# Prompt attention of a decoder step: inverse sums transposed and stored from GpSimd's queue, a third result buffer, operands prepared elsewhere in the half-step

## The chip, the cores and the metric

The kernel runs on one core of a Trainium2 chip. The metric is the device time of one execution in microseconds (us). TensorE (PE) multiplies and transposes, VectorE (DVE) and ScalarE (ACT) read its results from PSUM, GpSimd (POOL) works on SBUF, and DMAs are issued from the queues of SyncE (SP) and POOL.

## The reference

One step of a two-layer decoder for two groups that share the weights: a prompt of 1024 positions and 8 samples of 8 positions with a paged cache. Layer 0 is a pooling mixer and latent attention with 8 heads, then an MLP; layer 1 is a gated linear recurrence, then an MLP. The change touches the attention of layer 0. For the prompt it computes, for each of 8 heads with 96 elements per query and key:

```
s = (einsum(qn, k_nope) + einsum(qr, k_rope)) * 96 ** -0.5
s = where(key_pos <= query_pos, s, -inf)
p = softmax(s)
out = (p @ c) @ w_uv
```

All of it in float32. The samples have the same attention over 2048 cached positions each and 8 new ones.

## The kernel before, in words

Float32 accuracy comes from splitting each operand into a high and a low part of a narrower matmul type (`split`, L79 and L80) and adding three products (`mm3`, L136; the score and value products have their own loops).

`prompt_attention` works on 32 pieces, each a head h and a pair of query blocks ip, in the order 3, 0, 2, 1 within a head. Each piece takes two half-steps t, so a head takes eight, x = t % 8. The order of instructions on PE, DVE, ACT and POOL is the order in which this code issues them (`manual_schedule`); SP's queue is ordered by a scheduler. A half-step issues, in this order:

- `weigh`: ACT's exponential of the scores of the half-step before, L767, with the row sums written into `sm`.
- `prep` of the next head, in half-steps x = 4 to 7: four PE transposes of query or key rows into a bank `qkt`, ACT's high part (qth, L727, or kth, L730) and DVE's low part (ktl, L731). Part 0 also splits the head's values on POOL, `vt`, and, for every second head, issues from SP the loads of the query and key rows `qh` and `kh` (L691, L692) of the two heads after.
- `scores`: PE's score matmuls into one of two PSUM tiles `s` (L749), the causal mask (L752), and DVE's negated row maximum `nmx` (L755).
- `transposes` of earlier weights: PE (`ptp`, L794), ACT's high part `pTh` (L798), DVE's low part `pTl` (L799).
- `values`: PE's products with the values into `po` (L821), and, when a piece is complete, ACT's copy into the head's result buffer `ao` (L827), 128 x 1024. Its lower 64 partitions hold the high part's product and its upper 64 the low part's, which are to be added. There are two buffers `ao`.
- At x = 1, `inverses` of the head before: DVE's reciprocal `ri` of the row sums (L773), a DMA from SP that writes it to DRAM (`rs_d`, L774; its elements are not next to each other in DRAM), and a DMA from SP that reads it back, broadcast to all partitions (`rib`, L776).
- At x = 5, `finish` of the head before: POOL multiplies `ao` by `rib` (L780), SP stores the first 64 partitions into `mix_d` (L782), and POOL's queue adds the other 64 to the same rows by an accumulating DMA (L783), which waits for the store.

After the last head `sample_attention` begins: PE transposes the samples' queries and absorbs the key weights into them; `q4`, four copies of the rotary part of q, is made by POOL (L929) and transposed by PE (`q4t`, L934); a block-diagonal `qbd` is zeroed by POOL (L931) and filled by DVE (L936); POOL writes the mask `msk` of the new keys (L950 to L952), and DVE adds it to their scores (`snew`, L956). Then the cache is worked through page by page (128 pages): SP loads a page (`cp`, L892), PE transposes it (`cpt`, L973), DVE splits off its low part (`cl`, L977), PE forms the keys (`pk`, L136), and ACT copies its rotary scores (L1007).

Of the kernel before, what the change touches and what calls it, by code (L numbers as in the profile page):

```python
# [10 lines left out]
F32 = mybir.dt.float32  # L11
# [4 lines left out]
ALU = mybir.AluOpType  # L16
# [4 lines left out]
P = 128  # L21
D = 1024
KB = 8
SEQ = 1024
DB = 8
DT = 8
NS = DB * DT
# [3 lines left out]
H = 8  # L31
QN = 64
QR = 32
QH = 96
VH = 64
# [650 lines left out]
def load_heads(g, S, pl, hp, bufs):  # L686

    qt = pl.tile([P, 8, 2 * QH], F32, name="qh", tag="qh", bufs=bufs)
    kt = pl.tile([P, 8, 2 * QH], F32, name="kh", tag="kh", bufs=bufs)
    cols = slice(hp * 2 * QH, (hp + 1) * 2 * QH)  # L690
    g.nc.sync.dma_start(qt, S.q_d[:, cols].rearrange("(b p) d -> p b d", p=P))  # L691
    g.nc.sync.dma_start(kt, S.k_d[:, cols].rearrange("(b p) d -> p b d", p=P))  # L692
    return qt, kt


def prompt_attention(g, I, S, v_sb, first, mix0):
    nc = g.nc
    with ExitStack() as st:
        at = st.enter_context(pool(g, "at", 2, side="right"))
        ps = st.enter_context(pool(g, "ps3", space=PSUM))  # L700
# [5 lines left out]
        loaded = {0: first}  # L706
        heads = {}
        vts = {}
        ao = {}

        def prep(h, part):
            if part == 0:
                vt = vts[h] = at.tile([P, 8, 2, VH], F32R, name="vt", tag="vt")
                split(g, vt[:, :, 0], vt[:, :, 1], v_sb[:, :, h], nc.gpsimd)
                if h % 2 == 0 and h // 2 + 1 < 4:
                    loaded[h // 2 + 1] = load_heads(g, S, at, h // 2 + 1, 2)
                heads[h] = [at.tile([P, SEQ], F32R, name=nm, tag=nm) for nm in ("qth", "qtl", "kth", "ktl")]
            nm, hf = part // 2, part % 2
            src = loaded[h // 2][nm]
            th, tl = heads[h][2 * nm:2 * nm + 2]  # L720
            pt = ps.tile([P, 512], F32, name="qkt", tag="pt", bufs=3)
            for j in range(4):
                nc.tensor.transpose(pt[:QH, j * P:(j + 1) * P], src[:, hf * 4 + j, (h % 2) * QH:(h % 2 + 1) * QH], g.ident)
            cs = slice(hf * 512, (hf + 1) * 512)
            if nm == 0:

                nc.scalar.activation(th[:QH, cs], pt[:QH], AF.Copy, scale=SCALE)  # L727
                nc.vector.scalar_tensor_tensor(tl[:QH, cs], pt[:QH], SCALE, th[:QH, cs].bitcast(F32), ALU.mult, ALU.subtract)
            else:
                nc.scalar.copy(th[:QH, cs], pt[:QH])  # L730
                nc.vector.tensor_tensor(tl[:QH, cs], pt[:QH], th[:QH, cs].bitcast(F32), ALU.subtract)  # L731
# [27 lines left out]
        sums = {}  # L759
        rib = {}  # L760

        def weigh():
            h, i, sv, nm, nk = exps.pop(0)
            if h not in sums:
                sums[h] = g.tiny.tile([P, 8], F32, name="sm", tag="sm", bufs=2)
            p_ = at.tile([P, SEQ if i > 3 else 512], F32, name="p", tag="p" if i > 3 else "p4")
            nc.scalar.activation(p_[:, :nk], sv, AF.Exp, bias=nm, accum_out=sums[h][:, i:i + 1])  # L767
            P_[(h, i)] = p_

        def inverses(h):  # L770

            ri = g.tiny.tile([P, 8], F32, name="ri", tag="ri", bufs=2)
            nc.vector.reciprocal(ri, sums.pop(h))  # L773
            nc.sync.dma_start(S.rs_d[h].rearrange("(b p) -> p b", p=P), ri, allow_slow_non_contiguous=True)  # L774
            rib[h] = at.tile([P, SEQ], F32, name="rib", tag="rib", bufs=1)
            nc.sync.dma_start(rib[h], S.rs_d[h:h + 1].to_broadcast([P, SEQ]))  # L776

        def finish(h):
            o = ao.pop(h)
            nc.gpsimd.tensor_tensor(o, o, rib.pop(h), ALU.mult)  # L780
            rows = S.mix_d[512 + h * VH:512 + (h + 1) * VH, :SEQ]
            nc.sync.dma_start(rows, o[:VH])  # L782
            nc.gpsimd.dma_start(rows, o[VH:], accum_op=ALU.add)  # L783

        def transposes(h, ip, banks):

# [19 lines left out]
        def values(h, ip, banks):  # L806

            for b in banks:
                if b > ip:
                    continue  # L810
                if b == 0:
                    PO[h, ip] = ps.tile([P, 512], F32, name="po", tag="po", bufs=1)
                po = PO[h, ip]
                parts = PT.pop((h, ip, b))
                for jj in range(2):
                    j = 2 * b + jj
                    lone = j == 2 * ip + 1
                    out = po[:, P:2 * P] if lone else po[:, :2 * P]
                    cs = slice(2 * P, 3 * P) if lone else slice(jj * 2 * P, (jj + 1) * 2 * P)
                    for x, t in enumerate(parts):  # L820
                        nc.tensor.matmul(out, vts[h][:, j].rearrange("p s d -> p (s d)"), t[:, cs],  # L821
                                         start=(j == 0 and x == 0), stop=(lone and x == 1))
            if ip not in banks:
                return
            if h not in ao:
                ao[h] = at.tile([P, SEQ], F32, name="ao", tag="ao", bufs=2)
            nc.scalar.copy(ao[h][:, ip * 2 * P:(ip + 1) * 2 * P], PO.pop((h, ip))[:, :2 * P])  # L827

        for q in range(4):
# [3 lines left out]
        N = len(seq)  # L833
        ET = mybir.EngineType
        with g.tc.manual_schedule(engines={ET.PE, ET.DVE, ET.Activation, ET.Pool}):
            for t in range(2 * N + 6):
                n, half = divmod(t, 2)
                if exps:
                    weigh()
                if n < N:  # L840
                    h, ip = seq[n]
                    if h + 1 < H and n % 4 >= 2:
                        prep(h + 1, 2 * (n % 4 - 2) + half)
                    scores(h, 2 * ip + 1 - half)

                m, back = divmod(t - 3, 2)
                if 0 <= m < N:
                    transposes(*seq[m], (2, 3) if back else (0, 1))
                m, back = divmod(t - 4, 2)
                if 0 <= m < N:  # L850
                    values(*seq[m], (2, 3) if back else (0, 1))
                hd, x = divmod(t, 8)
                if x == 1 and hd:
                    inverses(hd - 1)
                elif x == 5 and hd:
                    finish(hd - 1)

def sample_attention(g, I, S, ahead, fill_start, fill):  # L860
    nc = g.nc
    SQ = H * DT
    with ExitStack() as st:
# [38 lines left out]
        pt = one("qst", "ct")  # L902
# [5 lines left out]
        for h0 in range(0, H, 2):  # L908
            pt = one("wkt", "up" if h0 % 4 else "dn", 2)
# [5 lines left out]
        for k in range(2):  # L915
            pt = one("qap", ("up", "dn")[k], 2)
# [9 lines left out]
            WQ.append(wq)  # L926

        q4 = sk.tile([P, H, 4, QR], F32, name="q4", bufs=1)
        nc.gpsimd.tensor_copy(q4[:NS], S.q_s[:NS, :, None, QN:].to_broadcast([NS, H, 4, QR]))  # L929
        qbd = sk.tile([P, DB, 4, H, DT], F32, name="qbd", bufs=1)  # L930
        nc.gpsimd.memset(qbd, 0.0)  # L931
        pt = msc("q4t")
        for h in range(H):
            nc.tensor.transpose(pt[:, h * NS:(h + 1) * NS], q4[:NS, h].rearrange("p a b -> p (a b)"), g.ident[:NS, :NS])  # L934
# [730 lines left out]
```

## Time and profile before

| | us |
|---|---|
| median of 3 runs | 2814.39 |
| lowest and highest | 2813.95, 2814.64 |
| the profiled execution | 2802.13 |
| its span | 2800.2 |

Over the span PE is busy 2670.9 us (95%), DVE 1771.8 (63%), ACT 923.6 (33%) and POOL 405.3 (14%). The prompt's attention is the part from 240 to 414 us.

In a timeline a row has the start, the length, the engine, the line, the operation with its output and inputs, the count, and in brackets the idle time of the engine before it and what ended that. PEld is PE's weight load. "SPq" and "POOLq" are queues' own rows. In a row of waits the numbers are the total, the count and the longest. PEclk is the granted clock of PE as a share of 2.4 GHz; 0.5 is its lower level of 1.2 GHz.

### The profile page before, as it was taken

What the parts mean: (1) busy time and instruction counts of PE and PEld (TensorE: products, weight loads), DVE (VectorE), ACT (ScalarE), POOL (GpSimd) and SP (SyncE); (2) the same over time, 40 slices, a digit from 0 to 9 for tenths busy, and PEclk for the clock granted to TensorE, in tenths of its full rate; (3) what the DMA queues carried; (4) which work ended last, traced back from release to release, by engine and by line L of the source; (5) the groups of instructions that cost most, each with busy time, mean ns of one, the idle gap of its engine ahead of it and who ended that gap; (6) DMA issues with size and microseconds to landing.
All of it is one profiled execution on the core that took longest, in us unless ns stands there. A gap on an engine that the chain in (4) does not pass through costs nothing.

```text
span 2800.2 us, 42502 instructions
## 1 busy us (share of the span) xinstructions
PE 2670.9 (95%) x16513; PEld 2584.3 (92%) x16513; DVE 1771.8 (63%) x3323; ACT 923.6 (33%) x1948; POOL 405.3 (14%) x459
## 2 busy tenths in 40 slices
PE   7998987999989999999999999999999999999999
PEld 6887877888879999999999988998999999999998
DVE  7666655788855555555555577997555555555555
ACT  5335764666644111111111135664411111111111
POOL 4221211322332000000000033444200000000000
PEclk9999998999999999999999999999999999999999
DMA  5233443222152111111111111113111111111101
GB/s 162 61 113 117 73 50 83 67 55 55 42 148 69 42 42 46 46 46 46 46 46 40 44 69 56 43 41 110 55 39 45 46 46 46 46 46 46 39 30 64
DMA packets 207859, 168.34 MB, mean 60 GB/s; under 512 B 48987, under 2 KB 189244, under 8 KB 206883
## 3 DMA queue, kind: packets, MB, share of 16 engines
q1 hardware_dynamic: 207019, 163.54, 19.7%
q0 software_dynamic: 640, 2.10, 1.2%
q8 instruction: 130, 2.13, 0.3%
q14 instruction: 70, 0.57, 0.1%
HBM read 142.37 MB, written 23.34 MB: 59 GB/s over the span
## 4 chain that ended last, share of the span: by engine, by line
PE 62%; DVE 7%; ACT 1%; DMA 1%; issue 1%; POOL 0%; ACTq 0%; DVEq 0%; POOLq 0%
PE up L136 27%; PE dn L136 26%; PE op L136 5%; PE pu L136 2%; DVE xl L182 1%; DVE v L1386 1%; PE pgt L136 1%; DVE ig L1401 1%; DVE hs L1417 0%; DMA raw<-mix_d 0%; DVE t L1402 0%; DVE y L250 0%; DVE ta L1404 0%; DVE xl L80 0%; PE otp L1596 0%
## 5 line engine op out<-in xcount | busy, mean ns | idle before, releaser
L250 DVE TENSOR_TENSOR y<-y,dn 128x384 f32<-128x384 f32 (+1 forms) x768 | 405.1, 531 | 282.1 <-PE dn L136 279.6
L136 PE MATMUL dn<-hh,whB 128*128 128x384 f32 (+1 forms) x1536 | 506.7, 330 | 3.9 <-DVE y L250 3.8
L136 PE MATMUL up<-xh,wlA 128*128 128x384 f32 (+1 forms) x1536 | 502.4, 327 | 0.0
L136 PE MATMUL dn<-hh,wlB 128*128 128x384 f32 (+1 forms) x1536 | 501.9, 327 | 0.0
L136 PE MATMUL up<-xh,whA 128*128 128x384 f32 (+1 forms) x1536 | 501.8, 327 | 0.0
L136 PE MATMUL up<-xl,whA 128*128 128x384 f32 (+1 forms) x1536 | 501.7, 327 | 0.0
L136 PE MATMUL dn<-hl,whB 128*128 128x384 f32 (+1 forms) x1536 | 501.6, 327 | 0.0
L79 ACT CAST whB<-raw 128x1024 fp32r<-128x1024 f32 (+3 forms) x80 | 80.0, 1035 | 699.5 <-PE dn L136 663.7
L136 PEld LDWEIGHTS dn<-hh,whB 128*128 128x128 f32 x1536 | 288.5, 188 | 11.9 <-DVE y L250 11.6
L136 PEld LDWEIGHTS up<-xh,wlA 128*128 128x128 f32 x1536 | 288.5, 188 | 0.4
L136 PEld LDWEIGHTS up<-xh,whA 128*128 128x128 f32 x1536 | 288.6, 188 | 0.3
L136 PEld LDWEIGHTS dn<-hl,whB 128*128 128x128 f32 x1536 | 288.6, 188 | 0.1
L136 PEld LDWEIGHTS up<-xl,whA 128*128 128x128 f32 x1536 | 288.5, 188 | 0.2
L136 PEld LDWEIGHTS dn<-hh,wlB 128*128 128x128 f32 x1536 | 288.6, 188 | 0.0
L235 DVE SCALAR_TENSOR_TENSOR rl<-up,rs 128x384 f32<-128x384 f32 (+1 forms) x192 | 102.8, 535 | 260.5 <-PE up L136 260.5
L236 ACT ACTIVATE hh<-rl 128x384 fp32r<-128x384 f32 (+1 forms) x192 | 97.1, 506 | 447.7 <-DVE rl L235 447.7
L80 POOL TENSOR_TENSOR wlA<-raw,whA 128x1024 fp32r<-128x1024 f32 (+2 forms) x24 | 58.1, 2422 | 745.8 <-ACT whA L79 745.8
L136 PE MATMUL pk<-wqh,cl 128*128 128x256 f32 (+1 forms) x512 | 153.3, 305 | 12.8 <-DVE cl L977 12.7
L136 PE MATMUL pk<-wqh,ch 128*128 128x320 f32 (+1 forms) x512 | 160.0, 315 | 0.7 <-ACT ch L976 0.7
L79 ACT CAST whA<-raw 128x1024 fp32r<-128x1024 f32 (+2 forms) x94 | 98.0, 1043 | 181.5 <-PE up L136 143.2
L237 DVE TENSOR_TENSOR rl<-rl 128x384 f32<-128x384 f32 (+1 forms) x192 | 106.0, 552 | 77.4 <-ACT hh L236 77.4
L136 PE MATMUL pk<-wql,ch 128*128 128x256 f32 (+1 forms) x512 | 151.8, 298 | 0.0
(561 smaller groups left out, 5324.8 us busy)
## 6 DMA issues: line engine op xcount, KB each, us to landing
raw<-in_w_up_dram SPq DMA_DIRECT2D x64, 512.0 KB
raw<-in_w_down_dram SPq DMA_DIRECT2D x64, 512.0 KB
cp<-in_cache_ckv_dram SPq DMA_DIRECT2D x128, 128.0 KB
raw<-in_w_in_rnn_dram SPq DMA_DIRECT2D x16, 512.0 KB
xt<-in_x_prompt_dram SPq DMA_DIRECT2D x8, 512.0 KB
raw<-in_w_out_even_dram SPq DMA_DIRECT2D x8, 512.0 KB
raw<-in_x_prompt_dram SPq DMA_DIRECT2D x8, 512.0 KB
rib<-rs_d SPq DMA_DIRECT2D x8, 512.0 KB
```

The costliest lines, as they stand in the source:

```text
L79: g.nc.scalar.copy(h, src)
L80: (lo or g.nc.vector).tensor_tensor(l, src, h.bitcast(F32), ALU.subtract)
L136: g.nc.tensor.matmul(ps, a, b, start=(i == 0), stop=(i == n - 1))
L182: nc.vector.scalar_tensor_tensor(xl[:, m], yv, gcol[:, m:m + 1], xh[:, m].bitcast(F32), ALU.mult, ALU.subtract)
L235: nc.vector.scalar_tensor_tensor(r[:, :n], ps[:, :n], 0.0, RS[c][:, :n], ALU.max, ALU.mult)
L236: nc.scalar.activation(hh[:, a:b], r[:, :n], AF.Square)
L237: nc.vector.tensor_tensor(r[:, :n], r[:, :n], r[:, :n], ALU.mult)
L250: nc.vector.tensor_tensor(y[c][:, m], y[c][:, m], ps[:, :n], ALU.add)
L1386: V.scalar_tensor_tensor(v, ul[:, a + k:b + k], vec[:, k, n:n + 1], v, ALU.mult, ALU.add)
L1401: V.scalar_tensor_tensor(t2, t2, 1.0, v, ALU.add, ALU.mult)
```

## The change

The inverse sums are transposed by PE into a bank `rit` of the PSUM tag that the other transposes use, copied out by DVE as `riT` (8 x 128), and written to DRAM from POOL's queue in rows of 128; the broadcast load of them is issued from POOL's queue too. `sm` and `ri` come from the loop's own pool. There are three buffers `ao`. `prep` of the next head stands at the end of half-steps x = 3 to 6, behind `values`, no longer ahead of `scores` in x = 4 to 7. The loads of query and key rows have one buffer each and are issued behind the last transposes of an odd head. `finish` stands at x = 4, and the accumulating DMA at x = 7; the last head's first store goes to POOL's queue as well. For the samples, the copy `q4` is made by ACT and `qbd` is zeroed by DVE.

```diff
--- before.py
+++ after.py
@@ -712,8 +712,6 @@
             if part == 0:
                 vt = vts[h] = at.tile([P, 8, 2, VH], F32R, name="vt", tag="vt")
                 split(g, vt[:, :, 0], vt[:, :, 1], v_sb[:, :, h], nc.gpsimd)
-                if h % 2 == 0 and h // 2 + 1 < 4:
-                    loaded[h // 2 + 1] = load_heads(g, S, at, h // 2 + 1, 2)
                 heads[h] = [at.tile([P, SEQ], F32R, name=nm, tag=nm) for nm in ("qth", "qtl", "kth", "ktl")]
             nm, hf = part // 2, part % 2
             src = loaded[h // 2][nm]
@@ -721,6 +719,8 @@
             pt = ps.tile([P, 512], F32, name="qkt", tag="pt", bufs=3)
             for j in range(4):
                 nc.tensor.transpose(pt[:QH, j * P:(j + 1) * P], src[:, hf * 4 + j, (h % 2) * QH:(h % 2 + 1) * QH], g.ident)
+            if part == 3 and h % 2 and h < H - 1:
+                loaded[h // 2 + 1] = load_heads(g, S, at, h // 2 + 1, 1)
             cs = slice(hf * 512, (hf + 1) * 512)
             if nm == 0:
 
@@ -762,25 +762,31 @@
         def weigh():
             h, i, sv, nm, nk = exps.pop(0)
             if h not in sums:
-                sums[h] = g.tiny.tile([P, 8], F32, name="sm", tag="sm", bufs=2)
+                sums[h] = at.tile([P, 8], F32, name="sm", tag="sm", bufs=2)
             p_ = at.tile([P, SEQ if i > 3 else 512], F32, name="p", tag="p" if i > 3 else "p4")
             nc.scalar.activation(p_[:, :nk], sv, AF.Exp, bias=nm, accum_out=sums[h][:, i:i + 1])
             P_[(h, i)] = p_
 
         def inverses(h):
 
-            ri = g.tiny.tile([P, 8], F32, name="ri", tag="ri", bufs=2)
+            ri = at.tile([P, 8], F32, name="ri", tag="ri", bufs=2)
             nc.vector.reciprocal(ri, sums.pop(h))
-            nc.sync.dma_start(S.rs_d[h].rearrange("(b p) -> p b", p=P), ri, allow_slow_non_contiguous=True)
+            pt = ps.tile([P, 512], F32, name="rit", tag="pt", bufs=3)
+            nc.tensor.transpose(pt[:8, :P], ri, g.ident)
+            riT = at.tile([8, P], F32, name="riT", tag="riT", bufs=1)
+            nc.vector.tensor_copy(riT, pt[:8, :P])
+            nc.gpsimd.dma_start(S.rs_d[h].rearrange("(b p) -> b p", p=P), riT)
+
+        def spread(h):
             rib[h] = at.tile([P, SEQ], F32, name="rib", tag="rib", bufs=1)
-            nc.sync.dma_start(rib[h], S.rs_d[h:h + 1].to_broadcast([P, SEQ]))
+            nc.gpsimd.dma_start(rib[h], S.rs_d[h:h + 1].to_broadcast([P, SEQ]))
 
         def finish(h):
             o = ao.pop(h)
             nc.gpsimd.tensor_tensor(o, o, rib.pop(h), ALU.mult)
             rows = S.mix_d[512 + h * VH:512 + (h + 1) * VH, :SEQ]
-            nc.sync.dma_start(rows, o[:VH])
-            nc.gpsimd.dma_start(rows, o[VH:], accum_op=ALU.add)
+            (nc.sync if h < H - 1 else nc.gpsimd).dma_start(rows, o[:VH])
+            return rows, o
 
         def transposes(h, ip, banks):
 
@@ -823,7 +829,7 @@
             if ip not in banks:
                 return
             if h not in ao:
-                ao[h] = at.tile([P, SEQ], F32, name="ao", tag="ao", bufs=2)
+                ao[h] = at.tile([P, SEQ], F32, name="ao", tag="ao", bufs=3)
             nc.scalar.copy(ao[h][:, ip * 2 * P:(ip + 1) * 2 * P], PO.pop((h, ip))[:, :2 * P])
 
         for q in range(4):
@@ -839,8 +845,6 @@
                     weigh()
                 if n < N:
                     h, ip = seq[n]
-                    if h + 1 < H and n % 4 >= 2:
-                        prep(h + 1, 2 * (n % 4 - 2) + half)
                     scores(h, 2 * ip + 1 - half)
 
                 m, back = divmod(t - 3, 2)
@@ -850,10 +854,15 @@
                 if 0 <= m < N:
                     values(*seq[m], (2, 3) if back else (0, 1))
                 hd, x = divmod(t, 8)
+                if hd + 1 < H and 3 <= x <= 6:
+                    prep(hd + 1, x - 3)
                 if x == 1 and hd:
                     inverses(hd - 1)
-                elif x == 5 and hd:
-                    finish(hd - 1)
+                    spread(hd - 1)
+                elif x == 4 and hd:
+                    done = finish(hd - 1)
+                elif x == 7 and hd or t == 2 * N + 5:
+                    nc.gpsimd.dma_start(done[0], done[1][VH:], accum_op=ALU.add)
 
 
 
@@ -926,9 +935,9 @@
             WQ.append(wq)
 
         q4 = sk.tile([P, H, 4, QR], F32, name="q4", bufs=1)
-        nc.gpsimd.tensor_copy(q4[:NS], S.q_s[:NS, :, None, QN:].to_broadcast([NS, H, 4, QR]))
+        nc.scalar.copy(q4[:NS], S.q_s[:NS, :, None, QN:].to_broadcast([NS, H, 4, QR]))
         qbd = sk.tile([P, DB, 4, H, DT], F32, name="qbd", bufs=1)
-        nc.gpsimd.memset(qbd, 0.0)
+        nc.vector.memset(qbd, 0.0)
         pt = msc("q4t")
         for h in range(H):
             nc.tensor.transpose(pt[:, h * NS:(h + 1) * NS], q4[:NS, h].rearrange("p a b -> p (a b)"), g.ident[:NS, :NS])
```

PE where half-step x = 1 ends and the next begins (`rit` is the transpose of the inverse sums of the head before). Before:

```order
L794 MATMUL ptp<-ident,p 128x128 x7
L821 MATMUL po<-pTh,vt 128x256
L821 MATMUL po<-pTl,vt 128x256
L821 MATMUL po<-pTh,vt 128x128
L821 MATMUL po<-pTl,vt 128x128
L749 MATMUL s<-kth,qth 128x256
L749 MATMUL s<-ktl,qth 128x256
```

Now:

```order
L800 MATMUL ptp<-ident,p 128x128 x7
L827 MATMUL po<-pTh,vt 128x256
L827 MATMUL po<-pTl,vt 128x256
L827 MATMUL po<-pTh,vt 128x128
L827 MATMUL po<-pTl,vt 128x128
L775 MATMUL rit<-ident,ri 8x128
L749 MATMUL s<-kth,qth 128x256
```

Between the values and the next scores there is now one transpose, which reads DVE's `ri`.

ACT in half-steps x = 6 and 7 (`kth` is the high part of the next head's keys, `p` the exponential). Before:

```order
L827 COPY ao<-po 128x256
L767 ACTIVATE p,sm<-s,nmx 128x640
L730 CAST kth<-qkt 96x512
L827 COPY ao<-po 128x256
L767 ACTIVATE p,sm<-s,nmx 128x512
L730 CAST kth<-qkt 96x512
L798 CAST pTh<-ptp 128x512 x2
```

Now:

```order
L833 COPY ao<-po 128x256
L730 CAST kth<-qkt 96x512
L767 ACTIVATE p,sm<-s,nmx 128x640
L833 COPY ao<-po 128x256
L730 CAST kth<-qkt 96x512
L767 ACTIVATE p,sm<-s,nmx 128x512
L804 CAST pTh<-ptp 128x512 x2
```

Each cast of `kth` has moved from behind an exponential to ahead of it.

POOL at the end of the prompt's attention and the start of the samples'. Before:

```order
L780 TENSOR_TENSOR ao<-ao,rib 128x1024
L783 DMA mix_d<-ao 64x1024
L929 COPY q_4781<-q_s 64x1024
L931 MEMSET qbd 128x2048
L950 MEMSET msk 64x64
```

Now:

```order
L778 DMA rs_d<-riT 8x128
L782 DMA rib<-rs_d 128x1024
L786 TENSOR_TENSOR ao<-ao,rib 128x1024
L788 DMA mix_d<-ao 64x1024
L865 DMA mix_d<-ao 64x1024
L959 MEMSET msk 64x64
```

The copy of q and the zeroing have left POOL's order, and the write of the inverses, their broadcast load and the last head's first store have come into it. On SP's queue the load of the page table (`ptb`) and those of the cache pages now stand directly behind the store of head 6.

## Rows read from the trace of the kernel before

**Rows 1.** Windows in prompt attention and at the start of the samples'.

```profile
core 0: us, PE busy (x) PEld busy (x) DVE busy (x) ACT busy (x) POOL busy (x), PEclk, DMA share, GB/s
...
308.00:329.00 21.00, 20.16 (x149) 17.52 (x148) 15.24 (x27) 16.31 (x39) 4.52 (x3) 1.00 0.31 59
415.00:436.00 21.00, 6.61 (x63) 6.22 (x61) 5.53 (x10) 4.49 (x10) 4.75 (x4) 0.66 0.28 51
436.00:450.00 14.00, 12.61 (x77) 11.18 (x76) 7.55 (x14) 5.97 (x19) 5.40 (x12) 0.65 0.41 106
```

**Rows 2.** Reciprocals of the row sums on DVE: summary of the line, then its timeline.

```profile
L773 DVE RECIPROCAL ri<-sm x8: 191/192/195, 265.4 to 413.8; 128x8 f32<-128x8 f32 x8
285.09 0.19 DVE L773 RECIPROCAL ri<-sm 128x8 f32<-128x8 f32 x1
308.84 0.19 DVE L773 RECIPROCAL ri<-sm 128x8 f32<-128x8 f32 x1
328.21 0.19 DVE L773 RECIPROCAL ri<-sm 128x8 f32<-128x8 f32 x1
347.60 0.19 DVE L773 RECIPROCAL ri<-sm 128x8 f32<-128x8 f32 x1
372.57 0.19 DVE L773 RECIPROCAL ri<-sm 128x8 f32<-128x8 f32 x1
```

**Rows 3.** Waits of ACT from 240 to 415 us: total, times, longest.

```profile
ACT ao L827 <- DMA mix_d<-ao: 15.8, 3, 5.7
```

**Rows 4.** Timelines of POOL, SP's queue and ACT around the first stall.

```profile
285.12 0.98 POOL L783 DMA_DIRECT2D mix_d<-ao  x1 [3.49 <-DMA mix_d<-ao]
285.31 0.38 SPq L774 DMA_DIRECT2D rs_d<-ri  x1
297.97 0.37 ACT L827 COPY ao<-po 128x256 f32<-128x256 f32 x1 [5.11 <-DMA mix_d<-ao]
```

**Rows 5.** POOL's accumulating stores, line 783: issue durations in ns, and landing.

```profile
L783 POOL DMA_DIRECT2D mix_d<-ao x8: 846/861/983, 285.1 to 433.6; - x8
DMA to landing us min/median/max: 3.9/7.1/12.7
```

**Rows 6.** Window behind the third stall.

```profile
404.70:411.60 6.90, 6.64 (x29) 6.33 (x30) 2.50 (x4) 4.16 (x11) 2.35 (x1) 0.51 0.34 97
```

**Rows 7.** Timeline of PE in an undisturbed head, half-step x = 1.

```profile
327.06 0.33 PE L749 MATMUL s<-kth,qth 96*128 96x256 f32 x1
```

**Rows 8.** Timelines of ACT, PE, weight loads, undisturbed head, x = 7 and 0.

```profile
339.83 0.69 ACT L767 ACTIVATE p<-s,nmx 128x512 f32<-128x512 f32 x1 [1.14 <-DVE nmx L755]
340.66 0.51 PE L749 MATMUL s<-kth,qth 96*128 96x512 f32 x1 [0.63 <-ACT p L767]
341.85 0.19 PEld L749 LDWEIGHTS s<-ktl,qth 96*128 96x128 f32 x1 [0.42 <-DVE ktl L731]
```

**Rows 9.** Timeline of ACT at the start of the loop.

```profile
251.00 1.05 ACT L79 CAST whA<-raw 128x1024 fp32r<-128x1024 f32 x1 [0.53 <-DMA raw<-in_w_out_even_dram]
```

**Rows 10.** Timelines of SP's queue, POOL, PE and DVE at the end.

```profile
414.00 0.37 SPq L774 DMA_DIRECT2D rs_d<-ri  x1
422.92 0.33 SPq L776 DMA_DIRECT2D rib<-rs_d  x1
427.85 2.33 POOL L780 TENSOR_TENSOR ao<-ao,rib 128x1024 f32<-128x1024 f32 x1 [14.48 <-DMA rib<-rs_d]
433.57 0.86 POOL L783 DMA_DIRECT2D mix_d<-ao  x1 [3.40 <-DMA mix_d<-ao]
435.54 1.11 PE L934 MATMUL q4t<-ident,q 64*128 64x64 f32 x8 [14.39 <-POOL q L929]
442.03 0.67 DVE L956 TENSOR_TENSOR snew<-snp,msk 64x512 f32<-64x512 f32 x1
```

**Rows 11.** Copy of the rotary scores, one per page of the cache.

```profile
L1007 ACT COPY s<-pk x128: 201/207/258, 446.2 to 766.5; 128x64 f32<-128x64 f32 x128
```

**Rows 12.** Timeline of POOL, a value split.

```profile
288.91 1.28 POOL L80 TENSOR_TENSOR vt<-v_sb,vt 128x512 fp32r<-128x512 f32 x1 [2.81 <-PE s L752]
```

## Prediction

> **What bounds the kernel now.** I read the page first (the slices, then the costliest groups), then the windows over prompt attention, the waits of ACT in it, the timelines of the engines at four places, and the queue waits. In an undisturbed head TensorE is the bound: in 21.0 us PE is busy 20.16, DVE 15.24, ACT 16.31, at full clock [rows 1]. A head then takes 19.4 us, read from one reciprocal of the row sums to the next: 328.21 − 308.84 = 19.37 and 347.60 − 328.21 = 19.39 [rows 2]. Two heads are longer, 308.84 − 285.09 = 23.75 and 372.57 − 347.60 = 24.97. There ACT's copy of the result waits for a DMA: three such waits, 15.8 us in all [rows 3], one of them 5.11 us [rows 4]. That is the wait for the result buffer of the head before last, whose accumulating store is still going. The store that delays it was issued at 285.12, beside the write of the inverse sums at 285.31 [rows 4], which goes out as 1024 single elements; the same pairing stands at the other two. POOL's accumulates land after 3.9 us at the least and 12.7 at the most [rows 5].
>
> At the end, after the last head, PE idles 14.39 us for POOL's copy of q [rows 10]. POOL is late because a chain of transfers stands before that copy: inverse sums out at 414.00, broadcast issued at 422.92, multiply at 427.85, accumulate at 433.57. The clock sinks there: granted 0.66 from 415 to 436 and 0.65 from 436 to 450 (1.0 is 2.4 GHz, 0.5 is 1.2) [rows 1].
>
> **The change part by part.** Sums are made against the profiled execution of 2802.13 us; the median of the runs is 2814.39, 12.26 more, and I carry the same shift over.
>
> A, **the three ACT stalls go**, for two reasons at once: the third buffer gives each accumulate a whole head more, and the 1024-element write is replaced by an 8x128 one with rows of 512 B. The first two are worth the excess of their heads over 19.38: 4.37 + 5.59 us, clock loss included. The third falls in the last head, which prepares no successor, so there is no equal to compare. By the ratio of the first two (9.96 us for 15.8 − 5.7 = 10.1 us of wait) it is 5.6; at the upper end it is 5.7 and half of the 6.9 us that follow at half clock [rows 6], 9.1. I take 6.7, nearer to the measured ratio. A = −16.6, ends −14 (buffers free somewhat late still) and −19.
>
> B, **PE waits for the reciprocal.** The transpose of the inverses stands on PE behind the values and ahead of the next scores. On a clean head PE began those scores at 327.06 [rows 7], while DVE's reciprocal began at 328.21 and took 0.19 [rows 2]: PE would stand until 328.40, so 1.3 us, eight times at most. The last of them stands ahead of work for the samples that may be late anyway: 0.8. The transpose itself is one short matmul, nothing beside this. B = 7 × 1.3 + 0.8 = +9.9. Ends: +4, where half is taken out of waits that PE has in the same head (21.0 − 20.16 = 0.84 per window), and +13, where copies behind it on DVE come 0.4 later each time. DVE's copy of 8x128 is no longer than its reciprocal row, since PE doesn't wait for it.
>
> C, **operands prepared at the end of half-steps.** ACT's cast of a half of kth now stands ahead of the exponential. Before, that exponential waited 1.14 us for DVE's maximum, and the cast came after it; so PE stood 0.63 for the scores' bank and its weight load 0.42 for ktl [rows 8]. Both holes, 1.05 us, should close, in 7 heads, −7.4; with a little from the queries' half I take −7.7. Ends: 0 (the hole moves to the maximum of the scores) and −9. The moved loads of query and key rows run while PE works, and have more than half a head before their first use: nothing, and a late one would show as a wait of PE's transposes.
>
> D, **the start.** ACT's first cast of the output weights, which waited 0.53 us for its load [rows 9], now stands ahead of the first copies of transposed weights: +1, ends 0 and +2.5 (the wait and two casts of 1.05).
>
> E, **the junction.** The copy of q goes to ACT, the zeroing to DVE, both idle there. The 14.39 us of PE's wait go. What is late next: the first page's latent rows, whose loads SP can now issue during the last head, since no write of that head is on its queue. Low end: the 10.7 us from 435.54 [rows 10] to the first page's output at 446.2 [rows 11] run at full clock too and take half, −14.4 − 5.3 = −19.7. High end: without a pause of its own PE goes three pages at half clock, each 2.52 us longer ((766.5 − 446.2)/127 [rows 11]), −14.4 + 7.6 = −6.8. I take −14.0, nearest to the wait that is measured.
>
> F, **POOL's and SP's queues.** Per head POOL now has 3.9 for the write of inverses (the least of its landings [rows 5], as no element-wise write is beside it), 4.93 from issue of the broadcast to the multiply, 2.33, 3.40 for the store, 0.86 for the accumulate [rows 10] and 1.28 for the value split [rows 12]: 16.7 us of 19.4. It fits, so it costs nothing; SP loses two issues and two long waits per head.
>
> Sum: −16.6 + 9.9 − 7.7 + 1.0 − 14.0 = −27.4; 2802.1 − 27.4 = 2774.7 profiled, and 2814.4 − 27.4 = **2787.0** for the median.
>
> **Rivals.** 1: *the order's gain does not come and PE's wait is longer* (C = 0, B = +13): −16.6 + 13 + 1 − 14 = −16.6, 2797.8. For it: PE has only 0.84 us of slack per window, so each hole that opens is paid for. Against: both holes of rows 8 end with instructions that the new order puts earlier.
>
> 2: *DVE stands at the mask.* The mask of the new keys is set by POOL, now behind the last head's whole chain; DVE's masked sums, at 442.03 before [rows 10], need it and stand ahead of the next split of latent rows. With F's terms the mask comes 17 us after the last reciprocal (413.8), and the sums' turn comes after PE's 7.4 us (435.54 − 14.39 = 421.15, less 413.79) and three pages of 2.5 to 5 us, so 16 to 24 after it: no wait or 1. If the write took the 8.92 us of before (422.92 − 414.00), the mask would be 5 later: up to +5, 2791.
>
> 3, the slower side: *POOL falls behind.* Its last chain ends at 265.4 [rows 2] + 8 × (time per head). Over (442.0 − 265.4)/8 = 22.1 us per head DVE's masked sums come later than they did before, and the kernel is slower. Were the write and the broadcast each to land in the 12.7 us that POOL's slowest accumulate took [rows 5], a head would take 12.7 + 12.7 + 2.33 + 3.40 + 0.86 + 1.28 = 33.3, the chain would end at 532, some 90 us late: 2904. Against it: the slow landings stand beside element-wise writes, which are gone; and POOL's eight issues took 846 to 983 ns [rows 5] while DVE was busy 15.24 of 21 us.
> The Trainium skill speaks for this rival ("SBUF — State Buffer", sections "SBUF: two separate sides" and "A bandwidth-pool intuition that's wrong"): a DMA issued from GpSimd's queue needs its descriptors written by GpSimd, which is shut out while VectorE runs an instruction in a two-port mode; the page measures 620 ns alone and 3100 ns beside such a copy, and advises SP's or ACT's queue. By that, an estimate from the page is 2.5 us more for each of three issues, 24.2 per head, past the point of 22.1 and about +17 us. The trace does not agree so far: its eight issues spread over 0.14 us.
>
> 4: *the stalls only move*, because the multiply and store come later with a slower chain: A = 0, so −10.8, 2803.6; with rival 1 on top it is 0, no change.
>
> **Chances.** Forecast 0.58, rival 1 0.19, rival 2 0.12, rival 3 0.05, rival 4 alone 0.03, with rival 1 0.03. A difference under 0.2% (5.6 us) can't be told from none here. Faster: 0.58 + 0.19 + 0.12 + 0.03 = 0.92, same 0.03, slower 0.05. The range goes up past rival 1 to 2802, and down by 14 of the 16.3 us that the low ends add up to (A 2.4, B 5.9, C 1.3, D 1.0, E 5.7), as all of them at once are unlikely: 2773. That leaves out rivals 3 and 4 and the far ends.
>
> **What would show it.** In the new profile: no wait of ACT's result copy for a DMA (A); a PE wait of about 1.3 us for the reciprocal in each head, and heads of 19.4 + 1.3 − 1.1 = 19.6 us (B, C); no hole of PE at the two scores of rows 8 (C); PE going on within 2 us of the last values, q's transposes without a wait for POOL (E); accumulates landing in about 4 us and POOL's multiply within 10 us of the reciprocal (F). Heads near 21 us mean rival 1; a DVE wait for the mask, rival 2; ACT waits for the accumulate that return in later heads, rival 3 or 4. Wrong altogether it is if the masked sums run later than 442 us.

## The result and the profile after

The changed kernel takes 2777.69 us (median of 4 runs, 2772.78 to 2778.56) against 2814.51 before (2813.95 to 2814.70): a ratio of 0.9866, 95% interval 0.9849 to 0.9883, or 36.8 us less. The forecast was 27.4 less, 2787.0 with a range of 2773 to 2802: the direction and the range held, the size was a quarter short. The profiled execution of the changed kernel took 2777.03 us, as the timed ones do.

The reciprocals of the row sums in the changed kernel, the summary of the line (compare [rows 2]):

```profile
L773 DVE RECIPROCAL ri<-sm x8: 193/194/195, 266.3 to 397.1; 128x8 f32<-128x8 f32 x8
```

and four of them in DVE's timeline:

```profile
285.48 0.20 DVE L773 RECIPROCAL ri<-sm 128x8 f32<-128x8 f32 x1
304.69 0.19 DVE L773 RECIPROCAL ri<-sm 128x8 f32<-128x8 f32 x1
323.86 0.20 DVE L773 RECIPROCAL ri<-sm 128x8 f32<-128x8 f32 x1
343.02 0.19 DVE L773 RECIPROCAL ri<-sm 128x8 f32<-128x8 f32 x1
```

The six heads that prepare a successor take 19.17 us each (343.02 − 323.86 is 19.16, 304.69 − 285.48 is 19.21), and the last, which prepares none, 15.79; no long head is left. From the first reciprocal to the last it is 397.15 − 266.31 = 130.8 us, where it was 148.3.

The waits of PE in the changed kernel, from 230 to 445 us: total, times, longest:

```profile
PE rit L775 <- DVE ri L773: 10.7, 8, 1.4
PE ptp L800 <- DVE pTl L805: 5.2, 1, 5.2
PE pk L136 <- DVE wql L80: 3.7, 1, 3.7
PE s L749 <- ACT p L767: 1.6, 2, 1.2
```

The new wait for the reciprocal is there eight times, 1.33 us each. The wait for the scores' bank, 4.7 us in seven before, is 1.6 in two. The 14.39 us for POOL's copy of q [rows 10] are gone; in their place stand 3.7 for DVE's low part of the key weights. One more wait, 5.2 us at the start, belongs to ACT, whose timeline there shows it:

```profile
248.01 1.04 ACT L79 CAST whA<-raw 128x1024 fp32r<-128x1024 f32 x1 [5.36 <-DMA raw<-in_w_out_even_dram]
```

ACT stands 5.36 us for the output weights, where it stood 0.53 [rows 9]. Its waits list has no row any more for a result copy that waits for the accumulate [rows 3]. The accumulates in the view of their line (issue in ns, then landing):

```profile
L865 POOL DMA_DIRECT2D mix_d<-ao x8: 887/893/899, 281.3 to 411.6; - x8
...
DMA to landing us min/median/max: 3.9/4.1/4.4
```

and the new write of the inverses in that of its own:

```profile
L778 POOL DMA_DIRECT2D rs_d<-riT x8: 556/562/709, 267.6 to 398.4; - x8
...
DMA to landing us min/median/max: 1.6/2.5/3.5
```

All eight accumulates land within 4.4 us, where three took over 10 and the slowest 12.7 [rows 5].

At the end of the prompt's attention, the timeline of PE:

```profile
405.54 0.71 PE L943 MATMUL q4t<-ident,q 64*128 64x64 f32 x8
412.75 0.90 PE L136 MATMUL pk<-wql,ch 128*128 128x320 f32 x2 [3.70 <-DVE wql L80]
```

that of DVE:

```profile
421.95 0.68 DVE L965 TENSOR_TENSOR snew<-snp,msk 64x512 f32<-64x512 f32 x1
```

and the copies of the rotary scores, one per page (compare [rows 11]):

```profile
L1016 ACT COPY s<-pk x128: 202/207/260, 417.7 to 738.1; 128x64 f32<-128x64 f32 x128
```

PE transposes q without a wait, 8.4 us after the last reciprocal (405.54 − 397.15). The first page is done 20.55 us after it (417.7 − 397.15), where it took 446.2 − 413.8 = 32.4 [rows 2, 11]. DVE's masked sums don't wait for the mask.

**The profiled execution of before was a short one.** From it to the profiled execution of after the time falls by 25.1 us only, while the medians differ by 36.8. So the kernel before was profiled twice more:

> The kernel before, unchanged, profiled again. Theory (the profiled execution of 2802 had fewer stalls than the timed ones of 2807 to 2816): one with 2808 to 2815 shows four to six waits of ACT's result copy for the accumulate, about 5 us each, in place of three. Rival: three waits again, and the time lies in other parts, as PE's clock in the MLPs.

> The same once more. Theory and rival as for the first: the time goes with the number of waits of ACT's result copy, or it doesn't.

They took 2814.46 and 2813.62 us, as the timed runs do. The theory was wrong: ACT's waits for the accumulate are 16.6 us in three and 18.1 in four, hardly more than the 15.8 of [rows 3], and from the first reciprocal to the last it is 148.3 and 148.0 us again. In the first of the two, the reciprocals:

```profile
L773 DVE RECIPROCAL ri<-sm x8: 192/194/195, 269.8 to 418.1; 128x8 f32<-128x8 f32 x8
```

the copies per page:

```profile
L1007 ACT COPY s<-pk x128: 203/207/259, 455.3 to 776.1; 128x64 f32<-128x64 f32 x128
```

ACT's timeline at the start and PE's at the end:

```profile
255.32 1.05 ACT L79 CAST whA<-raw 128x1024 fp32r<-128x1024 f32 x1 [2.06 <-DMA raw<-in_w_out_even_dram]
```

```profile
444.65 1.11 PE L934 MATMUL q4t<-ident,q 64*128 64x64 f32 x8 [18.67 <-POOL q L929]
```

The difference lies at both ends, not in the heads. The end is 455.3 − 418.1 = 37.2 us where [rows 2, 11] give 32.4, with a wait for q of 18.67 in place of 14.39; the first reciprocal is 4.3 us later, of which 2.7 were already there at a DVE row ahead of the loop (L564, 221.74 against 219.04) and 1.5 come from the longer wait for the output weights. Against this ordinary execution the change reads, in us:

| stretch | before, again | after | change | forecast |
|---|---|---|---|---|
| up to the first reciprocal | 269.8 | 266.3 | −3.4 | −0.1 (D, one head of C) |
| first reciprocal to last | 148.3 | 130.8 | −17.5 | −14.1 (A, six heads of C, seven of B) |
| last reciprocal to first page | 37.2 | 20.6 | −16.7 | −13.2 (E, the last of B) |
| the rest | 2357.3 | 2357.6 | +0.3 | 0 |
| span | 2812.6 | 2775.3 | −37.3 | −27.4 |

One of C's seven heads falls into the first stretch, because head 0 prepares head 1 before its own row sums are inverted.

### The profile page after: what moved, and what is told of

Same layout as the page of the kernel before. It is cut to its first block, busy times and chain, and to the rows that moved or that the text cites. A ratio compares the mean times of both kernels' runs of the same rounds, so it can differ in the third digit from the quotient of the medians.

```text
span 2775.3 us, 42539 instructions
## 1 busy us (share of the span) xinstructions
PE 2663.1 (96%) x16521; PEld 2580.4 (93%) x16521; DVE 1781.6 (64%) x3332; ACT 924.0 (33%) x1949; POOL 412.2 (15%) x474
## 3 DMA queue, kind: packets, MB, share of 16 engines
q1 hardware_dynamic: 197467, 159.05, 19.4%
## 4 chain that ended last, share of the span: by engine, by line
PE 64%; DVE 7%; ACT 1%; issue 1%; DMA 0%; POOL 0%; ACTq 0%; DVEq 0%; SPq 0%; POOLq 0%
PE up L136 27%; PE dn L136 27%; PE op L136 6%; PE pu L136 2%; DVE xl L182 1%; PE pgt L136 1%; DVE v L1395 1%; DVE ig L1410 1%; DVE hs L1426 0%; DVE y L250 0%; DVE t L1411 0%; PE pg L136 0%; DVE xl L80 0%; PE otp L1605 0%; DVE ta L1413 0%
## 5 line engine op out<-in xcount | busy, mean ns | idle before, releaser
L136 PEld LDWEIGHTS dn<-hh,whB 128*128 128x128 f32 x1536 | 288.3, 188 | 13.4 <-DVE y L250 13.1
L136 PE MATMUL pk<-wqh,cl 128*128 128x256 f32 (+1 forms) x512 | 153.6, 306 | 12.7 <-DVE cl L986 12.6
```

The lines of the kernel that those rows point to most:

```text
L136: g.nc.tensor.matmul(ps, a, b, start=(i == 0), stop=(i == n - 1))
```

## The experiments

Behind each time stand, in brackets, its ratio to the kernel before, which ran beside it, and the 95% interval of that ratio. The kernel before had medians of 2811.67 to 2812.59 us there, 2 to 3 us less than in the section on the result. So a difference to the changed kernel's 2777.69 us is uncertain by about 3 us, and the stretches of the traces are read with it. Of the longer edits only the lines that matter are shown; "..." marks what is left out.

**Two buffers or three.** The changed kernel with two result buffers.

```diff
-                ao[h] = at.tile([P, SEQ], F32, name="ao", tag="ao", bufs=3)
+                ao[h] = at.tile([P, SEQ], F32, name="ao", tag="ao", bufs=2)
```

> The changed kernel with two result buffers again. Theory (the form of the write removed the stalls): in the changed kernel head 0's accumulate is issued at 281.32 us and should land some 4 us later, while the buffer is next needed about 7.8 us after the second reciprocal (285.48), near 293; two buffers are enough, so no wait of ACT's result copy for a DMA and 2778 us, within 3. Rival (the third buffer removed them): waits of about 5 us come back in several heads, 2788 to 2808.

2777.17 us (0.9879, 0.9864 to 0.9894), the same as with three; no wait of ACT for the accumulate, heads of 19.1 us. Its accumulates:

```profile
DMA to landing us min/median/max: 3.9/4.2/4.7
```

With the new write the third buffer is worth nothing.

**The third buffer alone**, in the kernel before.

```diff
-                ao[h] = at.tile([P, SEQ], F32, name="ao", tag="ao", bufs=2)
+                ao[h] = at.tile([P, SEQ], F32, name="ao", tag="ao", bufs=3)
```

> The kernel before with a third result buffer and nothing else. Theory (either the buffer or the form of the write would have taken the stalls away): no wait of ACT's result copy for a DMA, heads of 19.4 us throughout, the end as before: 16 us less than before, 2797. Rival (the slow accumulates delay something else, the next loads or POOL's chain): the waits move, 2803 to 2813.

2796.58 us (0.9947, 0.9934 to 0.9960): 15 less than the 2811.67 of before beside it. All heads are 19.4 us, 398.0 − 267.1 = 130.9 in all, although the accumulates stay slow. The views of the accumulate's line, of the reciprocal's, and of PE's waits:

```profile
DMA to landing us min/median/max: 4.1/9.4/12.4
```

```profile
L773 DVE RECIPROCAL ri<-sm x8: 192/193/194, 267.1 to 398.0; 128x8 f32<-128x8 f32 x8
```

```profile
PE q4t L934 <- POOL q L929: 20.4, 1, 20.4
```

So either the buffer or the form of the write takes the stalls away, and either would have been enough. Of the 17.4 us that the heads lose, 1.3 come back at the end: the first page is done at 436.5, 38.5 us after the last reciprocal (37.2 in the kernel before, profiled again), and PE waits 20.4 for POOL's chain.

**The element-wise write kept**, with three buffers and without PE's transpose.

```diff
-            pt = ps.tile([P, 512], F32, name="rit", tag="pt", bufs=3)
-            nc.tensor.transpose(pt[:8, :P], ri, g.ident)
-            riT = at.tile([8, P], F32, name="riT", tag="riT", bufs=1)
-            nc.vector.tensor_copy(riT, pt[:8, :P])
-            nc.gpsimd.dma_start(S.rs_d[h].rearrange("(b p) -> b p", p=P), riT)
+            nc.sync.dma_start(S.rs_d[h].rearrange("(b p) -> p b", p=P), ri, allow_slow_non_contiguous=True)
...
-            nc.gpsimd.dma_start(rib[h], S.rs_d[h:h + 1].to_broadcast([P, SEQ]))
+            nc.sync.dma_start(rib[h], S.rs_d[h:h + 1].to_broadcast([P, SEQ]))
```

> The changed kernel, but the inverses go out as before: 1024 single elements and the broadcast load from SP's queue, no transpose on PE. Three result buffers stay. Theory (PE's wait for the reciprocal is paid in full): the eight waits of 1.33 us go, heads are 19.17 - 1.33 = 17.84 us, the slow accumulates come back but the third buffer hides them, 2767 us, within 4. Rival 1 (the write's form is what counts): ACT waits for the accumulate again in some heads, 2775 to 2785. Rival 2 (the mask): DVE's masked sums wait for POOL, whose chain ends some 5 us later; they had about 8 us of room, so nothing by the theory, up to 5 us by the rival.

2799.05 us (0.9960, 0.9946 to 0.9974): every expectation missed, 21 us over the changed kernel. The first two heads take 18.0 us, as the theory had it. Then PE waits for other transfers. PE's waits from 225 to 425 us and its timeline at the end:

```profile
PE qkt L721 <- DMA kh<-k_d: 7.3, 2, 4.2
```

```profile
425.56 0.69 PE L978 MATMUL cpt<-ident,cp 128*128 128x128 f32 x2 [17.12 <-DMA cp<-in_cache_ckv_dram]
```

The view of the accumulate's line:

```profile
DMA to landing us min/median/max: 4.4/9.9/12.2
```

SP's queue ahead of a pair of heads and at the end:

```profile
301.05 0.46 SPq L784 DMA_DIRECT2D mix_d<-ao  x1
301.60 0.54 SPq L692 DMA_DIRECT2D kh<-k_d  x1
...
417.36 0.33 SPq L778 DMA_DIRECT2D rib<-rs_d  x1
417.73 1.32 SPq L880 DMA_DIRECT2D ptb<-in_page_table_dram  x1
```

SP's queue is a line: the load of key rows stands behind a store that waits for POOL's multiply, which waits for the element-wise write; the page table's load stands behind the last broadcast load. With the slow write on that line the loads come late; that the single buffer for the rows adds to it is likely, but no run shows it. The line alone is not the cause: the next variant has the row-wise write on SP's queue, and its heads are not longer.

**The other issuing queue.** The changed kernel with the write, the broadcast and the last store issued from SP.

```diff
-            nc.gpsimd.dma_start(S.rs_d[h].rearrange("(b p) -> b p", p=P), riT)
+            nc.sync.dma_start(S.rs_d[h].rearrange("(b p) -> b p", p=P), riT)
...
-            nc.gpsimd.dma_start(rib[h], S.rs_d[h:h + 1].to_broadcast([P, SEQ]))
+            nc.sync.dma_start(rib[h], S.rs_d[h:h + 1].to_broadcast([P, SEQ]))
...
-            (nc.sync if h < H - 1 else nc.gpsimd).dma_start(rows, o[:VH])
+            nc.sync.dma_start(rows, o[:VH])
```

> The changed kernel with the transposed write, its broadcast load and the last head's first store issued from SP's queue in place of GpSimd's. Theory (who issues doesn't change how a transfer runs, but what stands behind it): heads stay at 19.2 us; at the end the load of the page table stands behind the last store, some 11.5 us after the last reciprocal, the first page then lands near 17 us after it where PE wants it at 8, so 9 to 12 us more, 2787 to 2790. Rival (the Trainium skill's rule on GpSimd's queue in the pages on SBUF decides: transfers of GpSimd start late beside VectorE): heads become shorter and the chain from reciprocal to multiply falls well under 8.6 us; 2770 to 2778.

2785.22 us (0.9903, 0.9889 to 0.9916), 7.5 more than the changed kernel, a little under the theory's 9 to 12. Heads are 19.2 us as in it, and the first page comes 427.2 − 400.45 = 26.8 us after the last reciprocal, 6.2 later; at the start ACT waits 6.97 us for the output weights in place of 5.36. The accumulates land in 3.8 to 4.8 us, so it is the form of the write, not its queue, that slowed them in the variant before this one. SP's queue at the end, then POOL's timeline and PE's waits:

```profile
402.68 0.32 SPq L782 DMA_DIRECT2D rib<-rs_d  x1
408.73 0.46 SPq L788 DMA_DIRECT2D mix_d<-ao  x1
409.23 0.45 SPq L884 DMA_DIRECT2D ptb<-in_page_table_dram  x1
```

```profile
406.36 2.35 POOL L786 TENSOR_TENSOR ao<-ao,rib 128x1024 f32<-128x1024 f32 x1 [9.00 <-DMA rib<-rs_d]
```

```profile
PE cpt L982 <- DMA cp<-in_cache_ckv_dram: 7.7, 1, 7.7
```

From the last reciprocal (400.45) to the multiply it is 5.9 us here, against 405.77 − 397.15 = 8.6 with POOL's queue. The two transfers are done 2.7 us sooner from SP, but PE doesn't wait for them, and what stands behind them on SP costs more.

**The copy of q back on POOL**, in the changed kernel.

```diff
-        nc.scalar.copy(q4[:NS], S.q_s[:NS, :, None, QN:].to_broadcast([NS, H, 4, QR]))
+        nc.gpsimd.tensor_copy(q4[:NS], S.q_s[:NS, :, None, QN:].to_broadcast([NS, H, 4, QR]))
...
-        nc.vector.memset(qbd, 0.0)
+        nc.gpsimd.memset(qbd, 0.0)
```

> The changed kernel with the copy of q and the zeroing of its block-diagonal back on GpSimd, behind the last head's chain. Theory: the copy ends near 16.5 us after the last reciprocal, so PE's transposes of q start some 8 us later than in the changed kernel (405.54 - 397.15 = 8.4 after it), the zeroing 2 us later still; 2786 to 2790. Rival (PE has other work to put there, or its pause was the clock's): 2778.

2783.41 us (0.9900, 0.9885 to 0.9914), 5.7 more, below the theory's 8. The first page comes 424.8 − 398.4 = 26.4 us after the last reciprocal, 5.9 later. PE waits:

```profile
PE q4t L943 <- POOL q L938: 7.5, 1, 7.5
```

**That move alone**, in the kernel before (the same two lines the other way).

> The kernel before with only the copy of q moved to ACT and the zeroing to DVE. Theory: the last head's chain and SP's order stay, so the load of the page table stands behind the last store, at 430.7, and the first page's rows land near 437: PE's wait for q becomes one for the page; of the 14.4 us some 0 to 2 are gained, 2810 to 2814. Rival (the wait for q was the whole price of the end): 14 less, 2798.

2816.52 us (1.0014, 1.0005 to 1.0023): nothing gained, and 2.5 us above the theory's range. The profiled execution, 2821.45, is the slowest of the eleven. PE's timeline at the end:

```profile
447.39 0.69 PE L973 MATMUL cpt<-ident,cp 128*128 128x128 f32 x2 [21.09 <-DMA cp<-in_cache_ckv_dram]
```

PE's wait for q has become a wait of 21.09 us for the first page, which is done 457.8 − 418.6 = 39.2 us after the last reciprocal. Together with the two runs before, this splits the end, which fell from 37.2 to 20.6 us. With the new write, either SP's order or the copy left as it was keeps a wait of 7.5 to 7.7 us and an end of 26.4 to 26.8. With the old write and order, moving the copy gains nothing. SP's order alone was not tried in the kernel before.

**The preparation where it was**, in the changed kernel.

```diff
                     h, ip = seq[n]
+                    if h + 1 < H and n % 4 >= 2:
+                        prep(h + 1, 2 * (n % 4 - 2) + half)
                     scores(h, 2 * ip + 1 - half)
...
-                if hd + 1 < H and 3 <= x <= 6:
-                    prep(hd + 1, x - 3)
```

> The changed kernel with the next head's operands prepared where they were before, ahead of the scores in half-steps x = 4 to 7. Theory: heads go back to 19.38 + 1.33 = 20.7 us, 1.54 more in each of seven, 2788 us, with PE's two holes (0.63 for the scores' bank, 0.42 for the key's low part) back. Rival (the order is worth nothing, heads are 19.17 for another reason): 2778.

2786.18 us (0.9911, 0.9895 to 0.9926), 8.5 more. Heads are (408.3 − 269.0 − 15.8)/6 = 20.6 us, and PE's wait for the scores' bank is back, as is its weight load's for `ktl` (3.0 us in seven, 0.4 at the longest):

```profile
PE s L749 <- ACT p L767: 5.7, 9, 1.2
```

The undisturbed head, 20.53 us, is the 19.38 of before with 1.15 added, and the order is worth 20.53 − 19.17 = 1.36 us a head.

**The reciprocal half a step earlier.** DVE's reciprocal at the end of x = 0, the transpose at the end of x = 1.

```diff
-                if x == 1 and hd:
-                    inverses(hd - 1)
-                    spread(hd - 1)
+                if x == 0 and hd:
+                    inverses(hd - 1)
+                elif x == 1 and hd:
+                    turn(hd - 1)
+                    spread(hd - 1)
```

> The changed kernel with DVE's reciprocal one half-step earlier (end of x = 0) and the transpose where it was (end of x = 1). Theory: PE's wait for the reciprocal, 1.33 us in each of eight heads, goes, heads are 17.9 us, 2767 us. Rival (PE has the slack elsewhere, the pace is set by DVE or ACT): the wait moves to another PE row, heads stay at 19.2, 2776 to 2779.

The lines that split `inverses` into the reciprocal and `turn`, which holds the transpose, the copy and the write, are not shown. 2769.53 us (0.9846, 0.9832 to 0.9859; runs of 2764.9 to 2770.0, all under those of the changed kernel), 8.2 less. Heads take 18.0 us, and the transpose's row has no wait:

```profile
265.52 0.27 PE L780 MATMUL rit<-ident,ri 128*8 128x128 f32 x1
```

Of the 1.33 us a wait, 1.15 is gained per head.

**Two waits more.** With that, the transposes of q and the second set of key weights behind the first page's preparation (`begin(0)` and `transp(0, 0)` first, then the two, each in a function of its own):

```diff
         begin(0)
         transp(0, 0)
+        rotary()
+        keyw(1)
```

> The variant with the early reciprocal, and at the start of the samples' attention the transposes of q, their four copies on DVE and the second set of key weights behind the first page's preparation. Theory: PE's wait of 3.0 us for DVE's low part of the key weights goes, so 3 us at half clock less than that variant's 2769.5: 2765 to 2768. Rival (the rotary product then waits for its operand): 2769 to 2773.

and, on top, the output weights behind the issue of a page in the middle of the first sample:

```diff
-                ahead(NJ - J)
+                with g.tc.issue_after(dmas[16]) if len(dmas) > 16 else nullcontext():
+                    ahead(NJ - J)
```

> The variant with the early reciprocal and the reordered start of the samples' attention, and the first output weights loaded and cast only when the samples' pages run. Theory: at the start of the prompt's loop ACT no longer stands 5.4 us for that load, PE's wait of 5.4 us there goes, 5 to 7 us less than that variant's 2765.9: 2759 to 2761. Rival (the casts take the same time from PE later, or the first weights come too late for the output projection): 2764 to 2768.

2765.86 us (0.9836, 0.9822 to 0.9850) and 2760.69 (0.9823, 0.9809 to 0.9836). In the first, PE's wait for the low part of the key weights is down from 3.0 to 0.2 us, and the first page comes 406.0 − 387.7 = 18.3 us after the last reciprocal. In the second, PE's wait of 5.4 at the start is gone, and the first reciprocal comes at 257.0 us, where it came at 264.2. Both medians are where the theories put them; the runs of the three variants overlap (2763.5 to 2767.4, 2758.3 to 2769.5), so the single steps rest on the traces more than on the times. The last is the fastest version here, 51 us under before.

Not tried by themselves were the later loads of query and key rows, the earlier `finish` with the later accumulate, and the new pool of `sm` and `ri`.

## Why the prediction was right, and where it was short

**A, the stalls: right, and over-explained.** They go. "For two reasons at once" is true in an exact sense that the prediction left open: each of the two does it alone. By the third buffer alone, the stalls between the reciprocals were worth 148.3 − 130.9 = 17.4 us, where 16.6 was forecast.

**B, PE's wait: right.** 1.3 us in eight was forecast, 10.7 in eight came. The variant with the early reciprocal shows that 1.15 of each is lost time.

**C, the order: right, a little too small.** −1.1 a head was forecast; undoing it costs 1.36. With B's 1.15 lost, a head is 19.38 + 1.15 − 1.36 = 19.17, where 19.6 was forecast. The three measured terms add up to what the heads lost: −17.4 + 7 × 1.15 − 6 × 1.36 = −17.5, where −14.1 was forecast.

**D, the start: wrong in sign.** The step was "+1, ends 0 and +2.5". ACT's wait for the output weights grew from 0.53 to 5.36 us, past the far end of the price. The load came sooner too, but the cast's turn more so: against the kernel before, profiled again, the load had landed at 248.01 us in place of 255.32, and ACT was ready for it at 242.65 in place of 253.26. Against this wait stood a term that the sum lacked. Before, ACT's first cast in the loop's pool waited for a store of another tile, in the timeline of the kernel before, profiled again:

```profile
237.57 0.62 ACT L79 CAST vt<-v_sb 128x512 fp32r<-128x512 f32 x1 [4.90 <-DMA out_dram<-so]
```

In the changed kernel that wait is gone; with the third buffer alone it is gone too, with only the copy of q moved it is not. The reading is that the pool's tiles now lie on memory with another last user; no trace shows addresses. The one gives 4.9, the other takes 5.36 − 2.06 = 3.3 against the ordinary execution.

But the first is worth nothing while the load stays late: with the third buffer alone ACT waits 5.50 us for the weights, and from ACT's copy `so` ahead of the loop (L579) to the first reciprocal it is 267.08 − 226.61 = 40.5 us, as in the kernel before (269.76 − 229.45 = 40.3). The changed kernel takes 266.31 − 229.12 = 37.2. There the loads of the next two heads' query and key rows no longer stand ahead of the output weights on SP, whose load is issued 10.2 us after that copy, where it was 14.6 with the third buffer alone. With the preparation put back it is 38.3, so 1.1 of the gain is C's. That the moved loads give the rest was not tried alone. The last variant, with the load out of the way, shows that ACT's wait is PE's time.

**E, the junction: right in kind.** −13.2 with B's last wait was forecast. Against the execution that it was worked out from, the end fell by 32.4 − 20.6 = 11.8; against the ordinary one by 16.7, as PE's wait for q was 18.67 there. What was said to be late next, the first page's rows, was not; DVE's low parts were, 3.7 us at a granted clock of 0.50 (409.0 to 412.7 us).

**F, the queues: right.** POOL's chain fits: the last accumulate's issue ends at 412.5 us, 15.4 after the last reciprocal, which is the sum of F's terms without the value split. Rival 3's slower side did not come, and no run made POOL fall behind. A queue did fall behind with the element-wise write back on SP, but it was SP's, and 21 us were lost.

**The step that failed most is the one ahead of the sum**: "I carry the same shift over". The 12.26 us between the profiled execution and the median were no constant overhead. Of the 12.4 us between the two spans (2812.6 − 2800.2), 4.8 lay in the end of this very stage and 1.5 in its start, where the change took them away; the other 6 or so lay ahead of the stage and behind it, and stayed. Those 6.3 us, with 17.5 − 14.1 = 3.4 in the heads, are nearly all of the 9.9 by which the forecast of the span fell short (37.3 against 27.4, 9.4 in the medians). Against the execution that the sum was worked out from the span fell by 24.9 us, 2.5 less than forecast. Rivals 1, 2 and 4 are refuted by the rows above: heads of 19.2, no wait for the mask, no wait for the accumulate. (Rival 2's price of up to 5 us makes 2792 by its own sum, not 2791; nothing hangs on it.)

The rule of the Trainium skill on GpSimd's queue ("SBUF — State Buffer", sections "SBUF: two separate sides" and "A bandwidth-pool intuition that's wrong") did not show in POOL's issues. The eight new writes were issued in 556 to 709 ns and landed in 1.6 to 3.5 us, with DVE busy three quarters of the time (the window of 308 to 329 us in the changed kernel):

```profile
308.00:329.00 21.00, 19.67 (x153) 17.68 (x151) 15.90 (x26) 16.42 (x39) 6.53 (x7) 1.00 0.24 52
```

No issue comes near the 3100 ns that the page measures for a DMA beside a VectorE copy. Which of DVE's instructions run in a two-port mode no trace shows, nor whether DVE has a part in the 2.7 us that the chain is longer from POOL's queue. The page's advice to issue from SP made the chain shorter and the kernel slower.

## What to carry to other kernels

A queue is a line: before a transfer is moved to the engine that runs it fastest, look at what is issued behind it and who waits for that. If the profiled execution is well off the timed ones, profile it again before taking durations from it, for the difference may lie in the stage that the change touches. A write of single elements is paid for by its neighbours: over these runs, accumulates in kernels with one took up to 13.4 us to land, in kernels without it 5.4 at most.

## What was not expected of the hardware

A change of one buffer's count took away a wait of 4.9 us for a store of another tile. Nothing in the code names that wait; that the pool's tiles moved in memory is the likely reason, and not shown. And the accumulates were slow by the company they kept: the same instruction, with the same 256 KB, landed in 3.9 to 4.4 us in the changed kernel and had a median of 9.9 where the single-element writes came back. Not each of them is slow: in the kernel before, one that was issued at 327.48 us, 0.95 ahead of such a write (328.43), landed in 4.2. What the two contend for no run shows.
